# A mixture of experts: most experts' rows fetched by indirect DMA, the adds of gathered rows placed later, and the overflow loop moved between two experts

## The chip, the cores and the metric

One core of one Trainium2 chip runs the whole program. Time is device microseconds of one execution, median of three: 3032.44 us for the kernel before. The kernel computes two blocks of two layers each; the change lies in the second block's mixture of experts (MoE), which runs twice, once a layer.

## The reference

What matters is `grouped_moe`. Each of 512 tokens picks a group of 4 experts and in it the top 2 of 16; each expert is a gated feed-forward net on its own tokens, and each token gets the weighted sum of its two results.

```python
g_idx = jnp.argmax(jnp.max(grouped, axis=-1), axis=-1)
top_vals, top_idx = lax.top_k(in_group, TOP_K)
experts = g_idx[:, None] * EXPERTS_PER_GROUP + top_idx
weights = top_vals / jnp.sum(top_vals, axis=-1, keepdims=True)
...
xb = x_pad[buf_tok].reshape(n_blocks, EXPERT_BLOCK, D)      # blocks of 128 rows, one expert each
h = jax.nn.silu(xblk @ w_gate[e]) * (xblk @ w_up[e])        # 1024 -> 512
y = h @ w_down[e]                                           # 512 -> 1024
...
x = layer_norm(DEEPNORM_ALPHA * x + f, ln2_g[l], ln2_b[l])
```

All is f32. An expert's three weight matrices are 2 MB each.

## The kernel before

Every f32 operand of a matmul is split in two parts of a narrower format (a high part and the rest), and each product is three matmuls (`mm3`, L184 to L186): high times high, high times rest, rest times high. ACT makes the high part by a copy (L108 to L112, for weights L1616), DVE the rest by a subtraction (L123 to L128, for weights L1617). The tiles are named wh, wl, mh, ml for weights, xgh, xgl for tokens, hh, hl for the hidden layer.

`moe` (L1677) works through one layer. `route` has given each token's rank in each expert's list (`rank`), its two slots (`slotf`), and the list of overflow blocks (`ovi`): an expert holds 128 tokens; what doesn't fit goes into further blocks. First `moe` issues the loads of expert 0's and a part of expert 1's weights. Then a loop over the overflow blocks (`tc.For_i`, L1688) runs a whole expert per block, its weights chosen by a register; in the shown runs it runs zero times in layer 0 and once in layer 1. All engines branch there together. Then come the 16 experts:

- `expert_slots` makes one-hot matrices (tokens by slots) for two experts at a time, on DVE for the first pair and on POOL for the others (L1650).
- `expert_in` (L1629) multiplies the split tokens by the one-hots: 64 matmuls of 128x256 (L1639) give the transposed tokens of two experts, which are split into xgh and xgl.
- `expert_up` (L1653): 24 matmuls for gate, silu on ACT (L1659), 24 for up, the product hs on DVE (L1661), four transposes (L1664) and a split into hh, hl.
- `expert_down` (L1668), one expert behind: 24 matmuls, two output copies yo on ACT, and two stores of 256 KB into `yd` in DRAM, on ACT's queue.

Expert 15's down isn't stored; its result is added straight from the chip through the matrix `ct` (L1770). For the others, eight indirect DMAs on POOL (L1751) gather each token's two rows from `yd` into yg tiles, and DVE adds them with their weights (`add`, L1760) into f, which is x at first; some are done on PE through diagonals (L1768). `combine` (L1771) finishes a row, and the norm follows.

Weights come in tiles of 512 KB (`wload`, L1602, names mr and wr, nine buffers in all) on SP's queue, issued as buffers come free. `wsplit` (L1606) splits each. Pools of buffers: `t2` (26 tiles in the MoE, the fourth number of T2) for hidden tiles, outputs and splits; `f4` for one-hots, the loop's weights and gathered rows. The order of instructions on each engine is set by a scheduler, which reads dependences, buffers and the marks of `issue_after`.

## Time and profile before

| | us |
|---|---|
| median of three runs (3029.88 to 3035.55) | 3032.44 |
| the profiled execution, its own time | 3038.98 |
| its span in the profile | 3037.2 |
| expert stage of layer 0, from expert 0's first gate matmul to the last products | 329.24 |
| expert stage of layer 1, likewise | 332.57 |

The mean granted clock of TensorE was 0.981 of full speed. The page's second part cuts the span into 40 slices of 76 us; layer 0's experts are slices 22 to 26, layer 1's slices 36 to 40. PE is TensorE's matmuls, PEld its weight loads, which run beside them.

### The profile page before, as it was taken

What the parts mean: (1) busy time and instruction counts of PE and PEld (TensorE: products, weight loads), DVE (VectorE), ACT (ScalarE), POOL (GpSimd) and SP (SyncE); (2) the same over time, 40 slices, a digit from 0 to 9 for tenths busy, and PEclk for the clock granted to TensorE, in tenths of its full rate; (3) what the DMA queues carried; (4) which work ended last, traced back from release to release, by engine and by line L of the source; (5) the groups of instructions that cost most, each with busy time, mean ns of one, the idle gap of its engine ahead of it and who ended that gap; (6) DMA issues with size and microseconds to landing.
All of it is one profiled execution on the core that took longest, in us unless ns stands there. A gap on an engine that the chain in (4) does not pass through costs nothing. (4 is left out here: it accounts for less than half of the span.)

```text
span 3037.2 us, 44080 instructions
## 1 busy us (share of the span) xinstructions
PE 2896.9 (95%) x16635; PEld 2454.0 (81%) x16635; DVE 1951.3 (64%) x3817; ACT 1557.7 (51%) x2717; POOL 271.0 (9%) x282
## 2 busy tenths in 40 slices
PE   8999999999999999999989999879999999699996
PEld 6888878876669998878888888669987878588874
DVE  4454467576656776444477878978744345777788
ACT  4343377466655455223345777535542244476774
POOL 0000000000000000000027000440000000260023
PEclk9999999999999999999999999989999999899998
DMA  4242325431026222322365988931223335378996
GB/s 133 85 148 81 105 84 160 141 91 36 25 84 205 70 60 66 97 88 80 103 201 196 330 320 322 320 98 59 64 78 96 90 111 167 112 277 302 326 324 239
DMA packets 335599, 453.48 MB, mean 149 GB/s; under 512 B 24374, under 2 KB 208408, under 8 KB 335384
## 3 DMA queue, kind: packets, MB, share of 16 engines
q1 hardware_dynamic: 320856, 421.78, 42.1%
q10 hardware_dynamic: 12224, 20.46, 1.8%
q0 software_dynamic: 2304, 8.39, 0.8%
q8 instruction: 132, 2.16, 0.3%
q14 instruction: 83, 0.68, 0.1%
HBM read 421.69 MB, written 28.88 MB: 148 GB/s over the span
## 5 line engine op out<-in xcount | busy, mean ns | idle before, releaser
L164 DVE TENSOR_TENSOR wl<-wr,wh 128x1024 fp32r<-128x1024 f32 x348 | 422.9, 1217 | 441.1 <-ACT wh L163 436.9
L163 ACT CAST wh<-wr 128x1024 fp32r<-128x1024 f32 x352 | 363.1, 1033 | 579.9 <-PE pj L185 336.6
L184 PE MATMUL pj<-x,wh 128*128 128x512 f32 x1288 | 508.2, 395 | 0.6 <-ACT x L110 0.6
L185 PE MATMUL pj<-x,wh 128*128 128x512 f32 x1288 | 507.6, 394 | 0.0
L186 PE MATMUL pj<-x,wl 128*128 128x512 f32 x1288 | 506.3, 393 | 1.1 <-DVE wl L164 1.0
L186 PEld LDWEIGHTS pj<-x,wl 128*128 128x128 f32 x1288 | 241.9, 188 | 54.9 <-issue 4.7
L184 PEld LDWEIGHTS pj<-x,wh 128*128 128x128 f32 x1288 | 242.0, 188 | 52.6 <-issue 4.6
L185 PEld LDWEIGHTS pj<-x,wh 128*128 128x128 f32 x1288 | 242.0, 188 | 52.3 <-issue 5.6
L211 PE MATMUL pj<-wh,x 128*128 128x256 f32 x864 | 249.1, 288 | 3.8 <-DVE xb L277 3.1
L212 PE MATMUL pj<-wl,x 128*128 128x256 f32 x864 | 247.2, 286 | 0.0
L213 PE MATMUL pj<-wh,x 128*128 128x256 f32 x864 | 245.3, 284 | 0.0
L211 PE MATMUL pj<-wh,yh 128*128 128x256 f32 x640 | 181.6, 284 | 0.5 <-ACT wh L163 0.3
L212 PE MATMUL pj<-wl,yh 128*128 128x256 f32 x640 | 179.6, 281 | 1.5 <-DVE wl L164 1.5
L213 PE MATMUL pj<-wh,yl 128*128 128x256 f32 x640 | 179.1, 281 | 0.4 <-DVE yl L127 0.3
L211 PEld LDWEIGHTS pj<-wh,x 128*128 128x128 f32 x864 | 166.3, 193 | 5.2 <-DVE xb L277 3.5
L212 PEld LDWEIGHTS pj<-wl,x 128*128 128x128 f32 x864 | 166.6, 193 | 0.4
L213 PEld LDWEIGHTS pj<-wh,x 128*128 128x128 f32 x864 | 166.3, 193 | 0.3
L1639 PE MATMUL pt<-oh,x 128*128 128x256 f32 x1088 | 136.2, 287 | 18.4 <-DVE oh L1695 8.6
L1617 DVE TENSOR_TENSOR wl<-mr,wh 128x1024 fp32r<-128x1024 f32 x106 | 139.1, 1312 | 22.3 <-ACT wh L1616 22.2
L1639 PEld LDWEIGHTS pt<-oh,x 128*128 128x128 f32 x1088 | 135.3, 195 | 20.2 <-DVE oh L1695 8.7
L1617 DVE TENSOR_TENSOR ml<-mr,mh 128x1024 fp32r<-128x1024 f32 x108 | 135.9, 1258 | 21.5 <-ACT mh L1616 19.4
L1419 POOL TENSOR_TENSOR x<-x,bc 128x512 f32<-128x512 f32 x14 | 18.2, 1321 | 1255.7 <-ACT x L1328 1255.7
(503 smaller groups left out, 6607.0 us busy)
## 6 DMA issues: line engine op xcount, KB each, us to landing
wr<-in_w_in SPq DMA_DIRECT2D x124, 512.0 KB, 3.7
mr<-in_w_exp_gate SPq DMA_DIRECT2D x76, 512.0 KB, 6.6
mr<-in_w_exp_up SPq DMA_DIRECT2D x72, 512.0 KB, 5.5
mr<-in_w_exp_down SPq DMA_DIRECT2D x66, 512.0 KB, 5.9
wr<-in_w_exp_down SPq DMA_DIRECT2D x62, 512.0 KB, 6.3
wr<-in_hawk_w_in SPq DMA_DIRECT2D x60, 512.0 KB, 3.6
wr<-in_w_exp_up SPq DMA_DIRECT2D x56, 512.0 KB, 4.4
wr<-in_w_exp_gate SPq DMA_DIRECT2D x52, 512.0 KB, 6.9
```

The lines of the kernel that those rows point to most:

```text
L163: self.nc.scalar.copy(wh[:, :kt, :c], raw[:, :kt, :c])
L164: eng.tensor_tensor(wl[:, :kt, :c], raw[:, :kt, :c], wh[:, :kt, :c].bitcast(F32), op=OP.subtract)
L184: mm(ps, a[0], b[0], start=first, stop=False)
L185: mm(ps, a[0], b[1], start=False, stop=False)
L186: mm(ps, a[1], b[0], start=False, stop=last)
L211: mm(d, tok(x[k][0]), w[k][0][:, :n], start=k == 0 and a == 0, stop=False, skip_group_check=True)
L212: mm(d, tok(x[k][0]), w[k][1][:, :n], start=False, stop=False, skip_group_check=True)
L213: mm(d, tok(x[k][1]), w[k][0][:, :n], start=False, stop=end, skip_group_check=True)
L1419: getattr(nc, eng[0]).tensor_tensor(t[v], x[v], gb[0][v], op=OP.mult)
L1617: self.nc.vector.tensor_tensor(wl, raw, wh.bitcast(F32), op=OP.subtract)
L1639: nc.tensor.matmul(pt[:, u * n:(u + 1) * n], xs[i][part][:, f], oh[:, i], start=i == 0 and part == 0, stop=i == 3 and part == 1)
```

## The change

Only experts 0 and 1 still get their tokens by one-hot matmuls. For the others:

- `after_mix` also stores each finished row tile of x into DRAM (`x1d`, eight stores of 256 KB a layer, by `put`, L541, on SP's queue).
- `slot_tokens` turns the ranks into a list idx: for each slot and expert, the token's number. It takes small DVE operations, two iotas on POOL and eight small bf16 matmuls.
- `expert_fetch` gathers an expert's 128 rows from `x1d` by one indirect DMA on POOL (512 KB, two buffers xg), issued two experts ahead.
- `expert_turn` transposes them, eight f32 transposes of 128x128, and splits them.

Expert 15's one-hot, which `ct` needs, is still made, for that one expert, on POOL. The loop over overflow blocks stands between experts 1 and 2. The adds of gathered rows for the first two row tiles are held behind `mark`, the last split before them (expert 15's hl). `t2` in the MoE has 22 buffers instead of 26.

```diff
--- before.py
+++ after.py
@@ -39,7 +39,7 @@
 
 G, V = ("gpsimd", "gpsimd"), ("vector", "vector")
 AFFINE = ((G, G), (G, G)), ((G, G), (G, V))
-T2 = (26, 29, 45, 26)
+T2 = (26, 29, 45, 22)
 
 
 def slopes(n):
@@ -1418,6 +1418,7 @@
                 with self.tc.issue_after(self.ranked.ins) if late else nullcontext():
                     getattr(nc, eng[0]).tensor_tensor(t[v], x[v], gb[0][v], op=OP.mult)
                     getattr(nc, eng[1]).tensor_tensor(t[v], t[v], gb[1][v], op=OP.add)
+            self.put(self.x1d[l], i0 + a, t)
             h, lo = [self.wp.tile([P, D], F32R, name="x1", tag="xt", bufs=8) for _ in range(2)]
             x1[i0 + a] = h, lo
             for v in range(2):
@@ -1465,6 +1466,7 @@
                 if j:
                     nc.vector.tensor_tensor(s, s, rb, op=OP.add)
         self.yd = self.dp.tile([SLOTS, D], F32, name="yd")
+        self.x1d = [self.dp.tile([T, D], F32, name=f"x1d{l}") for l in range(2)]
 
     def clear_slots(self):
 
@@ -1642,13 +1644,64 @@
             xT += [(h[:, u * n:(u + 1) * n], lo[:, u * n:(u + 1) * n]) for u in range(2)]
         return xT
 
-    def expert_slots(self, rank, e, eng):
-
-        oh = self.f4(F32R, "oh").rearrange("p (i a s) -> p i a s", i=4, a=2)
-        for a in range(2):
+    def expert_slots(self, rank, e, n, eng):
+
+        oh = self.f4(F32R, "oh")[:, :4 * n * P].rearrange("p (i a s) -> p i a s", i=4, a=n)
+        for a in range(n):
             for i in range(4):
                 eng.tensor_scalar(oh[:, i, a], self.iota, rank[:, i, e + a:e + a + 1], None, op0=OP.is_equal)
         return oh.rearrange("p i a s -> p i (a s)")
+
+    def slot_tokens(self, ohs, rank):
+
+
+        nc = self.nc
+        tt = nc.vector.tensor_tensor
+
+        tok = self.small([2, 4, 16], name="tok", bufs=1)
+        for u in range(2):
+            nc.gpsimd.iota(tok[:, u], pattern=[[u * P, 4], [0, 16]], base=0, channel_multiplier=1 - u,
+                           allow_small_or_imprecise_dtypes=True)
+        ps = self.pt()
+        a = self.small([4, 16], name="sta", bufs=1)
+        r = self.small([2, 4], name="str", bufs=1)
+        tk = self.small([2, 4, 2, 16], BF16, name="stk", bufs=1)
+        at = self.ph.tile([P, 2, 4, P], BF16, name="at", tag="t2", bufs=self.bufs["t2"])
+        for j, oh in enumerate(ohs):
+            tt(a, oh, rank, op=OP.mult)
+            nc.vector.tensor_reduce(r[:, j], a, axis=AX.X, op=OP.add)
+            for u in range(2):
+                tt(tk[:, j, :, u], oh, tok[:, u], op=OP.mult)
+            for i in range(4):
+                nc.vector.tensor_scalar(at[:, j, i], self.iota, r[:, j, i:i + 1], None, op0=OP.is_equal)
+        for j in range(2):
+            for i in range(4):
+                nc.tensor.matmul(ps[:, :32], at[:, j, i], tk[:, j, i].rearrange("p u e -> p (u e)"),
+                                 start=j == 0 and i == 0, stop=j == 1 and i == 3)
+        idx = self.small([16], I32, name="idx", bufs=1)
+        hi = self.small([16], name="idh", bufs=1)
+        nc.vector.tensor_copy(hi, ps[:, 16:32])
+        tt(idx, ps[:, :16], hi, op=OP.add)
+        return idx
+
+    def expert_fetch(self, l, idx, e):
+
+        xg = self.ph.tile([P, D], F32, name="xg", tag="xg", bufs=2)
+        self.nc.gpsimd.indirect_dma_start(out=xg, out_offset=None, in_=self.x1d[l],
+                                          in_offset=bass.IndirectOffsetOnAxis(ap=idx[:, e:e + 1], axis=0))
+        return xg
+
+    def expert_turn(self, xg):
+
+        xT = []
+        for h4 in range(2):
+            pt = self.pt()
+            for k in range(4):
+                f = (4 * h4 + k) * P
+                self.nc.tensor.transpose(pt[:, k * P:(k + 1) * P], xg[:, f:f + P], self.ident)
+            h, lo = self.split(pt, 1.0, "xg")
+            xT += [(h[:, k * P:(k + 1) * P], lo[:, k * P:(k + 1) * P]) for k in range(4)]
+        return xT
 
     def expert_up(self, xT, wg, wu):
 
@@ -1684,33 +1737,41 @@
 
         cur = self.small([P], name="cur", bufs=1)
         nc.vector.tensor_scalar(cur, self.iota, 16.0 * P - 1.0, None, op0=OP.add)
-        nov = nc.values_load(ovi[0:1, 7:8], min_val=0, max_val=N_OV)
-        with tc.For_i(0, nov, 1) as b:
-            ev = nc.values_load(ovi[0:1, bass.ds(b, 1)], engines=[mybir.EngineType.SP], min_val=0, max_val=15)
-            row = b * P + 16 * P
-            we = [w[bass.ds(ev, 1)].rearrange("o k c -> (o k) c") for w in W]
-            oh = self.f4(F32R, "oh").rearrange("p (i a s) -> p i a s", i=4, a=2)
-            for i in range(4):
-                nc.vector.tensor_scalar(oh[:, i, 1], cur, slotf[:, 0, i:i + 1], None, op0=OP.is_equal)
-                nc.vector.scalar_tensor_tensor(oh[:, i, 0], cur, slotf[:, 1, i:i + 1], oh[:, i, 1].bitcast(F32),
-                                               op0=OP.is_equal, op1=OP.add)
-            nc.vector.tensor_scalar(cur, cur, float(P), None, op0=OP.add)
-            xT = self.expert_in(xs, oh.rearrange("p i a s -> p i (a s)"), 256)
-            hT = self.expert_up([[v[:, :P] for v in t] for t in xT], self.wrows(we[0], 8, True), self.wrows(we[1], 8, True))
-            self.expert_down(hT, we[2], self.yd[bass.ds(row, P)], True)
-        oh = self.expert_slots(rank, 0, nc.vector)
-        xT = self.expert_in(xs, oh, 256)
+
+        def overflow():
+            nov = nc.values_load(ovi[0:1, 7:8], min_val=0, max_val=N_OV)
+            with tc.For_i(0, nov, 1) as b:
+                ev = nc.values_load(ovi[0:1, bass.ds(b, 1)], engines=[mybir.EngineType.SP], min_val=0, max_val=15)
+                row = b * P + 16 * P
+                we = [w[bass.ds(ev, 1)].rearrange("o k c -> (o k) c") for w in W]
+                oh = self.f4(F32R, "oh").rearrange("p (i a s) -> p i a s", i=4, a=2)
+                for i in range(4):
+                    nc.vector.tensor_scalar(oh[:, i, 1], cur, slotf[:, 0, i:i + 1], None, op0=OP.is_equal)
+                    nc.vector.scalar_tensor_tensor(oh[:, i, 0], cur, slotf[:, 1, i:i + 1], oh[:, i, 1].bitcast(F32),
+                                                   op0=OP.is_equal, op1=OP.add)
+                nc.vector.tensor_scalar(cur, cur, float(P), None, op0=OP.add)
+                xT = self.expert_in(xs, oh.rearrange("p i a s -> p i (a s)"), 256)
+                hT = self.expert_up([[v[:, :P] for v in t] for t in xT], self.wrows(we[0], 8, True), self.wrows(we[1], 8, True))
+                self.expert_down(hT, we[2], self.yd[bass.ds(row, P)], True)
+
+        oh = self.expert_slots(rank, 0, 2, nc.vector)
+        xT = [[[v[:, a * P:(a + 1) * P] for v in t] for t in xT] for xT in [self.expert_in(xs, oh, 256)] for a in range(2)]
+        idx = self.slot_tokens((oh1, oh2), rank)
+        fetched = {e: self.expert_fetch(l, idx, e) for e in (2, 3)}
         hT = None
         f = []
         for e in range(16):
-            if e % 2 == 0 and e < 14:
-                oh = self.expert_slots(rank, e + 2, nc.gpsimd)
-                nx = self.expert_in(xs, oh, 256)
+            if e == 2:
+                overflow()
+            if e == 12:
+                oh = self.expert_slots(rank, 15, 1, nc.gpsimd)
+            if 0 < e < 15:
+                xT.append(self.expert_turn(fetched.pop(e + 1)))
+                if e < 13:
+                    fetched[e + 3] = self.expert_fetch(l, idx, e + 3)
             if e == 15:
                 self.expert_down(hT, W[2][14], self.yd[14 * P:15 * P])
-            o = e % 2 * P
-            h2 = self.expert_up([[v[:, o:o + P] for v in t] for t in xT],
-                                *[self.wrows(W[j][e], 8, first=first.pop(0) if first else None) for j in range(2)])
+            h2 = self.expert_up(xT[e], *[self.wrows(W[j][e], 8, first=first.pop(0) if first else None) for j in range(2)])
             if e == 2:
                 slot, wv, wl = self.weigh(oh1, oh2, sc, slotf)
             if e == 13:
@@ -1725,17 +1786,15 @@
             if 0 < e < 15:
                 self.expert_down(hT, W[2][e - 1], self.yd[(e - 1) * P:e * P])
             hT = h2
-            if e % 2:
-                xT = nx
 
         pt = self.pt()
         for i in range(4):
-            nc.tensor.transpose(pt[:, i * P:(i + 1) * P], oh[:, i, P:].bitcast(F32), self.ident)
+            nc.tensor.transpose(pt[:, i * P:(i + 1) * P], oh[:, i].bitcast(F32), self.ident)
         ct = self.t2(F32R, "ct")
         nc.scalar.copy(ct, pt)
         pw = self.pt()
         for i in range(4):
-            nc.tensor.matmul(pw[:, :1], oh[:, i, P:].bitcast(F32), wl[:, i:i + 1], start=i == 0, stop=i == 3)
+            nc.tensor.matmul(pw[:, :1], oh[:, i].bitcast(F32), wl[:, i:i + 1], start=i == 0, stop=i == 3)
         dg = self.t2(F32, "dg")
         for i in range(2):
             for j in range(2):
@@ -1771,13 +1830,15 @@
                 nc.vector.tensor_tensor(f[i][h], f[i][h], ps, op=OP.add)
 
         y = []
+        mark = self.split_end[0]
         for c in range(2):
             py = self.pj()
             ws2 = list(self.wsplit(raws[c]))
             if c:
-                for i in range(2):
-                    for j in range(2):
-                        add(i, j)
+                with tc.issue_after(mark.ins):
+                    for i in range(2):
+                        for j in range(2):
+                            add(i, j)
             for k, wk in enumerate(ws2):
                 self.mm3(py, hT[k], wk, k == 0, k == 3)
                 if c == 1 and k == 1:
```

SP's queue around the loop, layer 0, before (mr, wr: weight tiles; rovi: the register that holds the loop's count):

```order
L1602 DMA mr<-in_w_exp_up 128x2x512
L160 DMA wr<-in_w_mem_kv 128x4x256 x7
L1602 DMA wr<-in_w_exp_up 128x2x512 x3
L1687 TENSOR_LOAD rovi
L1687 ISA x2
L1602 DMA wr<-in_w_exp_gate 128x2x512
L1688 COMPARE_AND_BRANCH
L1688 UNCONDITIONAL_BRANCH x2
```

and now:

```order
L1604 DMA wr<-in_w_exp_down 128x2x512
L1604 DMA mr<-in_w_exp_down 128x2x512
L1604 DMA wr<-in_w_exp_down 128x2x512
L1604 DMA mr<-in_w_exp_gate 128x2x512
L1604 DMA wr<-in_w_exp_gate 128x2x512 x2
L1604 DMA mr<-in_w_exp_gate 128x2x512
L1604 DMA wr<-in_w_exp_up 128x2x512
L1604 DMA mr<-in_w_exp_up 128x2x512 x3
L1604 DMA wr<-in_w_exp_down 128x2x512
L1743 COMPARE_AND_BRANCH
L1743 UNCONDITIONAL_BRANCH x2
```

Before, the branch stands behind the first tiles of experts 0 and 1. Now it stands behind all loads of experts 0 and 1 that have a place and nine tiles more, which belong to expert 2 and to the down of expert 1.

PE where the loop's body ends (the first rows are the body's last), layer 1, before (x with a number: the parts of the tokens):

```order
L186 MATMUL pj<-mh,hl 128x512
L1688 REGISTER_ALU
L1688 COMPARE_AND_BRANCH
L1688 UNCONDITIONAL_BRANCH
L1639 MATMUL pt<-oh,x_24627 128x256
L1639 MATMUL pt<-oh,x_24628 128x256
L1639 MATMUL pt<-oh,x_24641 128x256
```

and now:

```order
L186 MATMUL pj<-mh,hl 128x512
L1743 REGISTER_ALU
L1743 COMPARE_AND_BRANCH
L1743 UNCONDITIONAL_BRANCH
L1701 MATMUL pt<-ident,xg 128x128 x8
L184 MATMUL pj<-wh,xgh 128x512
L185 MATMUL pj<-wl,xgh 128x512
L186 MATMUL pj<-wh,xgl 128x512
```

Before, the one-hot matmuls of experts 0 and 1 follow the loop; now the transposes of expert 3's fetched rows and the gate of expert 2 do.

DVE at the end of layer 1's experts (hs and hl: expert 15; yg: gathered rows; rw: weights of tokens), before:

```order
L1617 TENSOR_TENSOR wl<-mr,wh 128x1024
L1617 TENSOR_TENSOR ml<-mr,mh 128x1024
L1661 TENSOR_TENSOR hs<-hs,pj 128x512
L1617 TENSOR_TENSOR wl<-wr,wh 128x1024
L1617 TENSOR_TENSOR ml<-mr,mh 128x1024
L125 TENSOR_TENSOR hl<-pt,hh 128x512
L1745 COPY ws<-pt 128x1
L1760 SCALAR_TENSOR_TENSOR x<-yg,rw,x 128x512 x5
```

and now:

```order
L1619 TENSOR_TENSOR ml<-wr,mh 128x1024
L1619 TENSOR_TENSOR wl<-mr,wh 128x1024
L1819 SCALAR_TENSOR_TENSOR x<-yg,rw,x 128x512
L1714 TENSOR_TENSOR hs<-hs,pj 128x512
L1619 TENSOR_TENSOR ml<-mr,mh 128x1024
L1619 TENSOR_TENSOR wl<-wr,wh 128x1024
L125 TENSOR_TENSOR hl<-pt,hh 128x512
L1804 COPY ws<-pt 128x1
L1619 TENSOR_TENSOR ml<-mr,mh 128x1024
L1819 SCALAR_TENSOR_TENSOR x<-yg,rw,x 128x512 x3
```

Before, all adds stand behind hs, hl and ws. Now one add of gathered rows stands ahead of hs, and the others as before behind it; the same holds in layer 0. This one belongs to the third row tile, which the mark doesn't hold.

## Rows read from the trace of the kernel before

**Rows 1.** The page: busy time by engine, and slices of PE and DMA.

```profile
PE 2896.9 (95%) x16635; PEld 2454.0 (81%) x16635; DVE 1951.3 (64%) x3817; ACT 1557.7 (51%) x2717; POOL 271.0 (9%) x282
...
PE   8999999999999999999989999879999999699996
...
DMA  4242325431026222322365988931223335378996
```

**Rows 2.** Windows of both expert stages: us, busy by engine, clock, DMA share, GB/s.

```profile
core 0: us, PE busy (x) PEld busy (x) DVE busy (x) ACT busy (x) POOL busy (x), PEclk, DMA share, GB/s
1634.18:1963.42 329.24, 324.11 (x1618) 268.88 (x1616) 270.36 (x254) 239.89 (x278) 63.10 (x47) 0.99 0.90 319
2671.06:3003.63 332.57, 325.94 (x1618) 270.51 (x1616) 270.39 (x254) 239.73 (x278) 65.96 (x52) 0.99 0.89 316
```

**Rows 3.** Timeline of ACT, silus of four experts: start, us, operation.

```profile
1676.18 0.60 ACT L1659 ACTIVATE hs<-pj 128x512 f32<-128x512 f32 x1 [0.33 <-PE pj L186]
1693.29 0.60 ACT L1659 ACTIVATE hs<-pj 128x512 f32<-128x512 f32 x1 [0.33 <-PE pj L186]
1717.94 0.60 ACT L1659 ACTIVATE hs<-pj 128x512 f32<-128x512 f32 x1 [0.33 <-PE pj L186]
1735.06 0.60 ACT L1659 ACTIVATE hs<-pj 128x512 f32<-128x512 f32 x1 [0.32 <-PE pj L186]
```

**Rows 4.** The page's group of L1639, and PE's timeline: eight transposes in layer 1.

```profile
L1639 PE MATMUL pt<-oh,x 128*128 128x256 f32 x1088 | 136.2, 287 | 18.4 <-DVE oh L1695 8.6
...
2595.78 1.07 PE L1497 MATMUL pt<-ident,x 128*128 128x128 f32 x8
```

**Rows 5.** Layer 0 at the loop: timelines of PE and DVE, and the loop's branches.

```profile
1612.06 0.28 PE L213 MATMUL pj<-wh,mx 128*128 128x256 f32 x1
1617.62 0.80 PE L1639 MATMUL pt<-oh,x 128*128 128x256 f32 x2 [5.28 <-ACT mh L1616]
...
1613.44 1.72 DVE L1650 TENSOR_SCALAR oh<-iota,rank 128x128 fp32r<-128x128 f32 x8 [4.08 <-ACTq L1688]
...
L1688 PEldq COMPARE_BRANCH  x6: 86/192/3861, 1610.8 to 2652.5; - x6
```

**Rows 6.** Timeline of PE in layer 1: the body's start and what follows it.

```profile
2619.09 8.28 PE L1639 MATMUL pt<-oh,x 128*128 128x256 f32 x48 [8.59 <-DVE oh L1695]
...
2653.89 6.38 PE L1639 MATMUL pt<-oh,x 128*128 128x256 f32 x35 [4.50 <-DVE oh L1650]
```

**Rows 7.** Timeline of ACT and DVE in layer 0: one weight tile's split.

```profile
1637.16 1.05 ACT L1616 CAST mh<-wr 128x1024 fp32r<-128x1024 f32 x1 [0.33 <-PE pj L186]
...
1638.24 1.23 DVE L1617 TENSOR_TENSOR ml<-wr,mh 128x1024 fp32r<-128x1024 f32 x1
```

**Rows 8.** DMA issues: count, KB each, median us to landing.

```profile
mr<-in_w_exp_gate SPq DMA_DIRECT2D x76, 512.0 KB, 6.6
...
yd<-yo ACTq DMA_DIRECT2D x62, 256.0 KB
```

**Rows 9.** Windows inside the expert stages, columns as in rows 2.

```profile
1676.18:1717.94 41.76, 41.76 (x217) 35.21 (x216) 33.49 (x33) 30.98 (x36) 0.00 (x0) 1.00 0.91 326
1720.00:1755.00 35.00, 35.00 (x188) 29.72 (x188) 28.86 (x29) 25.72 (x31) 0.00 (x0) 1.00 1.01 367
1815.00:1840.00 25.00, 25.00 (x143) 21.67 (x142) 19.23 (x19) 17.11 (x21) 0.00 (x0) 1.00 1.01 366
1925.00:1945.00 20.00, 20.00 (x90) 16.13 (x90) 15.61 (x15) 15.37 (x20) 0.00 (x0) 1.00 1.05 385
2860.00:2880.00 20.00, 20.00 (x121) 17.62 (x120) 15.13 (x16) 13.37 (x17) 0.00 (x0) 1.00 1.03 386
```

**Rows 10.** The indirect DMAs of L1751: ns on POOL (min/median/max), and landing.

```profile
L1751 POOL DMA_INDIRECT yg<-yd,rslot x16: 933/1014/2107, 1949.2 to 3004.4; - x16
...
DMA to landing us min/median/max: 5.2/5.8/8.3
```

**Rows 11.** Timelines of POOL and DVE: third gather and expert 15's hs, both layers.

```profile
2992.66 1.97 POOL L1751 DMA_INDIRECT yg<-yd,rslot  x1 [0.30 <-issue]
...
2994.06 0.69 DVE L1661 TENSOR_TENSOR hs<-hs,pj 128x512 f32<-128x512 f32 x1 [0.25 <-PE pj L186]
...
1953.58 0.94 POOL L1751 DMA_INDIRECT yg<-yd,rslot  x1 [0.30 <-issue]
...
1953.85 0.69 DVE L1661 TENSOR_TENSOR hs<-hs,pj 128x512 f32<-128x512 f32 x1 [0.25 <-PE pj L186]
```

## The prediction

> **What bounds the kernel now.** I read the page first: TensorE is busy for 95% of the span [rows 1]. The two expert stages are the two stretches in which DMA is busy too, digits 8 and 9 of slices 23 to 26 and 37 to 39. Next the windows by stage: each expert stage lasts about 330 us, PE works in all but 5 to 7 us of it, and the 16 DMA engines are busy 0.90 and 0.89 of it at 319 and 316 GB/s [rows 2]. So PE sets the end there, with the weight stream close behind. The starts of the silu of four experts in a row give the price of a step: 17.11 us when no one-hot group lies between two of them, 24.65 when one does [rows 3]. The 64 matmuls of expert_in for two experts thus cost 24.65 − 17.11 = 7.54 us of PE, all on the path.
>
> **What goes and what comes on PE.** Of 8 groups a layer the first (experts 0 and 1) stays and 7 go: 7 × 7.54 = 52.8 us. In their place come 14 expert_turn of 8 transposes of 128x128. The same shape took 1.07 us for 8 in layer 1 [rows 4], so 14 × 1.07 = 15.0. Net −37.8 a layer, **−75.6** in all. The transposes' weight loads lie beside them (PEld is busy less than PE, [rows 1]). The splits of xg need 2 ops of 512 columns per expert instead of 4 per pair: no change on DVE or ACT. POOL's one-hots go but for 4 ops a layer; nobody waited for them between the experts (PE stands 5 to 7 us in a whole stage, [rows 2]).
>
> **The loop, moved.** It now stands where a stream runs. Layer 0 skips it. Today the skip costs 5.28 us of idle PE between the last mem_kv matmul and the first L1639, 3.86 of which is PE's own branch [rows 5]; the one-hots of 1.72 us start in it. After, PE runs from mem_kv into expert_in but still waits some 1.5 us for one-hots: −3.8. At the new place PE drains (about 1.6: a copy of 0.6, as a silu of [rows 3], and 1 for the meeting at the branch, an estimate: the first matmul behind the body waited 4.50 in layer 1 for that meeting and its one-hots together, [rows 6]), branches (3.9), turns expert 3, and waits for the first split of weights, which ACT and DVE can't do ahead of their own branches: an ACT copy of 1.05 and a DVE op of 1.23, about 2.3 [rows 7]. Then it runs at the lower clock: after its gap the first 48 matmuls of L1639 in layer 1 took 8.28 us, 172 ns each against 7.54 / 64 = 118 between the experts [rows 6], for which I add 1. That is +8.8 − 3.8 = **+5** (bounds +1, branch and refill hidden, to +9, nothing saved at the top). In layer 1 the body runs once. It takes 34.8 us from 2619.09 to 2653.89 [rows 6] wherever it stands; the 4.50 us behind it, a wait for one-hots, turns into the refill; the drain and the entry come new: **+4** (+1 to +8). SP's nine prefetches (eight tiles of expert 2's gate and up and one of down 1) stand ahead of its branch, so the prefetch survives the loop.
>
> **The weight stream.** Behind the loop PE has 332.6 (layer 1's window, [rows 2]) − 52.8 − 28.5 (two ups and one down are 5/3 of 17.11, done before) + 13.9 (13 turns) = 265 us to do. The last tile may land some 8 us before its end (a split and one down), so it has 257, with the refill about 259. In that time go 163 tiles of 512 KB, 29 stores of 256 KB and 11 fetches of 512 KB: 163 × 0.524 + 29 × 0.262 + 11 × 0.524 = 98.8 MB [rows 8]. That is 381 GB/s, where today's mean is 319. Can DMA do it? In stretches where its share reaches 1 it moved 366 and 367, and 385 and 386 in the best 20 us [rows 9]. I take 372, nearer the longer stretches: 98.8 / 0.372 = 265.6, **+6** a layer, +12 in all (0 at 386; +19 a layer at 355, below). So the forecast is that DMA becomes the bound behind the loop, at 7.34 MB a step (12 tiles, 2 stores, a fetch) / 0.372 = 19.7 us, where PE alone would need 17.11 + 1.07 = 18.2.
>
> The Trainium skill ("DMA: Bandwidth & Descriptors", section "Where 436 GB/s comes from") says that for transfers between HBM and SBUF a limit of about 358 GB/s binds. At 358 the term above would be 98.8 / 0.358 = 276, +17 instead of +6 a layer. The trace shows 385 and 386 over 20 us [rows 9], which is more than that limit, so I don't use it. Another page of the Trainium skill ("HBM Reference", its first section) has a core that streams alone well above its share, at about 425; at that rate the term would be nothing, and no stretch of this trace shows it.
>
> **The fetches.** Two buffers and an issue two experts ahead give each fetch some 36 us; an indirect DMA of today is at most 2.1 on POOL and 8.3 to landing [rows 10]. Only the first is tight: its index needs slot_tokens (some 22 small DVE ops between splits, 8 small matmuls), and turn 2 stands right behind expert 0's hidden transposes, some 11 us into expert 0. I take +1.5 a layer (0 to +4), **+3**. The small ops themselves and the 8 stores of x1d on SP: +0.5 a layer, **+1** (0 to 4); SP's queue has nothing urgent behind those stores.
>
> **The tail.** Before, every add of gathered rows stood behind expert 15's hl split. After, the hoisted adds of tokens 0 and 1 are held behind it, but one of the others, the first gather of token block 2, now stands on DVE ahead of expert 15's hs multiply, in both layers. That gather is the third on POOL: issued at 2992.66, and 5.2 us or more to land [rows 10, 11], so 2997.9 at the earliest, while hs started at 2994.06. Behind the waiting add on DVE stand hs and its splits; PE waits for hs with its transposes and the last down. In layer 0 the third issue is at 1953.58 and hs at 1953.85 [rows 11]. The wait costs about 4.5 to 5.5, of which one add of 0.7 comes back and some is covered by PE's backlog: **+4** a layer (0 to +7), +8.
>
> **Sum.** −75.6 + 9 + 12 + 3 + 1 + 8 = −42.6. Against the profiled execution's own 3038.98 that is 2996.4; that execution stood 6.5 above the median, and on the median's scale 3032.44 − 42.6 = **2990**.
>
> **Rivals.** (A) DMA keeps up and PE stays the bound. For it: 385 and 386 have been reached, and nine tiles lie ahead. Without the 12 and with half of tail and fetch: −75.6 + 9 + 1 + 5.5 = −60, so 2972. (B) DMA settles lower: the whole stages moved 319 at a share of 0.90, and 319 / 0.90 = 354, 326 / 0.91 = 358 [rows 2, 9]. At 355: 98.8 / 0.355 = 278, +19 instead of +6 a layer, so 3016. The limit of about 358 that the Trainium skill states ("DMA: Bandwidth & Descriptors", "Where 436 GB/s comes from") would give 3012. (C) Slower: the stream behind the loop gets no more than today's mean, since stores, fetches and loads then share queues and the buffers come free in bursts. The place is experts 2 to 15, the price 98.8 / 0.326 − 259 = 44 a layer, so 3032.4 − 42.6 − 12 + 88 = 3066. It decides below the rate at which the gain is gone: 27.3 a layer to lose, 98.8 / (259 + 27.3) = 345 GB/s. Against it: every stretch with share 1 was above 360. (D) The change doesn't do what it says: the prefetch behind the loop or the fetches come late at every turn. 28 waits of 1.5 us would eat the 42, near 3030. The lead of 36 us speaks against it.
>
> **How the numbers follow.** Main case 0.57 (2975 to 3005), A 0.13, B 0.15, C 0.09, D 0.06. The range runs from 2964, A with nothing lost in the tail, to 3018, just above B; C, D and a little of the rest are outside. About 0.2%, 6 us, is what a measurement can tell from no change: faster by more 0.86 (main, A, B and a little of D), within it 0.05, slower 0.09.
>
> **What would show it.** L1639's successor should have 192 matmuls (two groups and the body's) instead of 1088 [rows 4], and L1701 224 transposes near 0.13 us each. The silu starts behind the loop tell the bound: 18.2 us a step is A, 19.7 is the forecast, 20.9 (today's pair divided by two, 41.76 / 2, [rows 9]) is no gain. In the window from the loop to the end, DMA's share should be near 1 at 370 GB/s and PE should wait for splits whose raw tile has just landed; if the share stays at 0.9 and PE still idles, another engine is the bound and the DMA term is wrong. PE should idle about 8 us at the loop in layer 0. In the tail the add ahead of hs should wait for a gather, 4 to 5 us; if hs isn't late, that term goes. PE waiting at many turns for xg would make the prediction wrong, as would a rate below 345 GB/s.

## The result

The changed kernel takes 2988.01 us, median of four runs (2980.78 to 2988.76), beside 3031.85 of the kernel before: a ratio of 0.9849 (0.9831 to 0.9867), 44 us less. In a second set of runs it had 0.9846 (0.9830 to 0.9862). The forecast was 2990. That it came so near is partly luck: three costs of its sum (the loop, the stream, the fetches) were too large and two (the transposes, the tail) too small, and the step that was to take 19.7 us takes 18.4 to 18.7.

The page of the changed kernel, to be read beside [rows 1], and windows inside layer 0's experts, beside [rows 9]:

```profile
span 2978.8 us, 42692 instructions
PE 2830.5 (95%) x15979; PEld 2369.2 (80%) x15979; DVE 1947.0 (65%) x3853; ACT 1543.0 (52%) x2713; POOL 199.0 (7%) x210
...
DMA  4242324431016312323266999832122334479995
```

```profile
core 0: us, PE busy (x) PEld busy (x) DVE busy (x) ACT busy (x) POOL busy (x), PEclk, DMA share, GB/s
...
1695.00:1760.00 65.00, 64.91 (x300) 52.24 (x299) 56.98 (x57) 51.99 (x63) 3.27 (x3) 1.00 1.05 393
1760.00:1855.00 95.00, 94.87 (x435) 74.92 (x434) 84.51 (x82) 77.80 (x93) 4.68 (x5) 1.00 1.05 393
1855.00:1900.00 45.00, 41.91 (x184) 31.90 (x182) 40.88 (x35) 33.21 (x41) 16.81 (x8) 1.00 0.99 362
```

PE lost 66 us of work. Where 326 GB/s went before, 393 go now for 160 us on end, at a share of 1.05, and PE still has no idle time there. The kernel before reached such a rate too, but only briefly. The 385 and 386 of [rows 9] are not its best 20 us; a window that begins a little before the last row there has more (columns as above):

```profile
2857.50:2877.50 20.00, 20.00 (x117) 17.39 (x116) 16.20 (x16) 14.58 (x18) 0.00 (x0) 1.00 1.04 394
```

In the last of the changed kernel's three windows PE stops for 3 us and the rate falls: that is the stretch in which POOL adds the two parts of x.

A table of the same stretches in three executions, from the starts of silus, of the routing's first small matmul, and the end of the last product of `ct`:

| us | before | changed | changed, second profile |
|---|---|---|---|
| layer 0: routing to expert 2's silu | 81.4 | 68.5 | 71.4 |
| expert 2's silu to expert 15's | 272.4 | 249.6 | 249.1 |
| expert 15's silu to the last product | 29.5 | 32.6 | 34.3 |
| layer 0's last product to layer 1's routing (the handover) | 632.0 | 631.7 | 632.4 |
| layer 1: routing to expert 2's silu | 103.0 | 94.7 | 94.4 |
| expert 2's silu to expert 15's | 275.7 | 251.4 | 253.0 |
| expert 15's silu to the end of the span | 48.5 | 60.1 | 59.0 |

The profiled execution of before stood 7.1 us above the median of 3031.85, the changed kernel's first 7.2 below its own, so their spans differ by 58.4 us, 14 more than the medians. The second profile (span 2984.7) stands nearer its own median of 2988.80. Differences of 2 or 3 us in one row are within what one build shows of itself.

Steps in the middle, to be read beside [rows 3] (timeline of ACT, experts 11 to 13 of layer 0):

```profile
1824.11 0.60 ACT L1712 ACTIVATE hs<-pj 128x512 f32<-128x512 f32 x1 [0.29 <-PE pj L186]
1842.73 0.60 ACT L1712 ACTIVATE hs<-pj 128x512 f32<-128x512 f32 x1 [0.27 <-PE pj L186]
1861.35 0.60 ACT L1712 ACTIVATE hs<-pj 128x512 f32<-128x512 f32 x1 [0.38 <-PE pj L186]
```

18.62 us each, where a pair took 41.77 before, 20.9 each. The three steps from expert 7 to 10 took 18.36 to 18.40.

The turn itself, where PE goes from an expert's down to the next gate (timeline of PE):

```profile
1798.31 0.39 PE L186 MATMUL pj<-mh,hl 128*128 128x512 f32 x1
1798.54 1.04 PE L1701 MATMUL pt<-ident,xg 128*128 128x128 f32 x8
1799.33 0.48 PE L184 MATMUL pj<-wh,xgh 128*128 128x512 f32 x1
1799.65 0.39 PE L185 MATMUL pj<-wl,xgh 128*128 128x512 f32 x1
```

The tail, beside [rows 11] (timeline of DVE, layer 0 and layer 1):

```profile
1917.52 1.00 DVE L1819 SCALAR_TENSOR_TENSOR x<-yg,rw,x 128x512 f32<-128x512 f32 x1 [5.24 <-DMA yg<-yd,rslot]
1918.44 0.68 DVE L1714 TENSOR_TENSOR hs<-hs,pj 128x512 f32<-128x512 f32 x1
...
2930.50 0.75 DVE L1819 SCALAR_TENSOR_TENSOR x<-yg,rw,x 128x512 f32<-128x512 f32 x1 [7.46 <-DMA yg<-yd,rslot]
2931.17 0.68 DVE L1714 TENSOR_TENSOR hs<-hs,pj 128x512 f32<-128x512 f32 x1
```

The add ahead of hs does wait for its gather, 5.24 and 7.46 us, and hs stands right behind it.

### The profile page after: what moved, and what is told of

Same layout as the page of the kernel before. It is cut to its first block, busy times and chain, and to the rows that moved or that the text cites. A ratio compares the mean times of both kernels' runs of the same rounds, so it can differ in the third digit from the quotient of the medians.

```text
span 2978.8 us, 42692 instructions
## 1 busy us (share of the span) xinstructions
PE 2830.5 (95%) x15979; PEld 2369.2 (80%) x15979; DVE 1947.0 (65%) x3853; ACT 1543.0 (52%) x2713; POOL 199.0 (7%) x210
## 3 DMA queue, kind: packets, MB, share of 16 engines
q1 hardware_dynamic: 323160, 425.98, 42.6%
## 5 line engine op out<-in xcount | busy, mean ns | idle before, releaser
L211 PE MATMUL pj<-wh,x 128*128 128x256 f32 x864 | 248.0, 287 | 1.5 <-DVE xb L277 0.7
L1619 DVE TENSOR_TENSOR ml<-mr,mh 128x1024 fp32r<-128x1024 f32 x108 | 134.0, 1242 | 26.3 <-ACT mh L1618 25.6
L1619 DVE TENSOR_TENSOR wl<-mr,wh 128x1024 fp32r<-128x1024 f32 x106 | 131.6, 1242 | 27.4 <-ACT wh L1618 27.2
L1618 ACT CAST mh<-mr 128x1024 fp32r<-128x1024 f32 x108 | 113.0, 1048 | 26.2 <-PE pj L186 9.8
L1618 ACT CAST wh<-mr 128x1024 fp32r<-128x1024 f32 x106 | 111.4, 1051 | 23.9 <-DMA mr<-in_w_exp_down 8.6
L212 PEld LDWEIGHTS pj<-wl,yh 128*128 128x128 f32 x640 | 121.2, 189 | 2.4 <-DVE wl L164 1.9
```

What stands on the lines that cost most here:

```text
L211: mm(d, tok(x[k][0]), w[k][0][:, :n], start=k == 0 and a == 0, stop=False, skip_group_check=True)
L212: mm(d, tok(x[k][0]), w[k][1][:, :n], start=False, stop=False, skip_group_check=True)
L1618: self.nc.scalar.copy(wh, raw)
L1619: self.nc.vector.tensor_tensor(wl, raw, wh.bitcast(F32), op=OP.subtract)
```

## Experiments

### Is the weight stream the bound? Twice the fetches, and almost none

The edit of double_fetch, in `expert_fetch`:

```diff
         self.nc.gpsimd.indirect_dma_start(out=xg, ..., in_offset=...(ap=idx[:, e:e + 1], axis=0))
+        self.nc.gpsimd.indirect_dma_start(out=xg, ..., in_offset=...(ap=idx[:, e:e + 1], axis=0))
```

> The changed kernel with every fetch of an expert's rows issued twice into the same buffer: 0.52 MB more per expert, nothing more for PE, DVE or ACT. Theory A, the weight stream is the bound in the steady experts, at 394 GB/s: a step goes from 7.34 MB / 394 = 18.6 us to 7.86 / 394 = 20.0, and the 10 or so steps of each layer that the tiles ahead don't cover give 10 to 14 us a layer, 20 to 30 in all, near 3013. At the rate that the prediction took, 372, a step would be 21.1. Theory B, PE is the bound and the step is 18.4 to 18.6 because the transposes cost more there than in layer 1's router: steps stay at 18.6 and the time within 4 us of 2988.

It took 3030.79 us, 0.9988 of before (0.9979 to 0.9997): nearly all of the gain is gone. A window in the middle of layer 0 (columns as above), and PE's timeline at its first turn:

```profile
1790.00:1860.00 70.00, 66.54 (x301) 50.86 (x300) 58.76 (x57) 53.40 (x64) 9.75 (x7) 1.00 1.05 395
```

```profile
1639.65 1.94 PE L1703 MATMUL pt<-ident,xg 128*128 128x128 f32 x8 [7.37 <-DMA xg<-x1d,idx]
```

The seven steps from expert 6 to 13 take 19.2 to 20.7 us, 19.9 on the mean, and the rate is 395 GB/s. So the stream runs at its own limit, and a step that moves 7.86 MB is as long as that takes. Theory A holds for the steps, in mechanism and number: from expert 2's silu to 15's a layer takes 12 us more. Its total, near 3013, is missed by 18 us, because it left out the start. The second row shows that: the first turn (the eight transposes of `expert_turn`) waits 7.37 us for its doubled fetch, and the start grows by 8 to 12 us a layer. In the changed kernel this first fetch just comes in time: the step from expert 0 to 1 is 11.57, that is 10.60 of before and a turn, and in its second profile the first turn of layer 0 waits 0.33.

reuse_rows leaves out the rows of experts 4 to 15:

```diff
-                xT.append(self.expert_turn(fetched.pop(e + 1)))
-                if e < 13:
-                    fetched[e + 3] = self.expert_fetch(l, idx, e + 3)
+                xT.append(self.expert_turn(fetched[2 + (e + 1) % 2]))
```

> The changed kernel without the fetches of experts 4 to 15: their transposes read the rows of experts 2 and 3 again, so the rows of 12 experts are left out and their results are those of other tokens. PE, DVE and ACT do the same work; 0.52 MB less moves per expert. Theory A, the stream at 394 GB/s binds: 6.82 / 394 = 17.3 us a step is less than PE's own, so steps fall from 18.6 to 18.2, by 3 to 5 us a layer, 6 to 10 in all, near 2980. Theory B, PE binds: steps stay at 18.4 to 18.6 and the time within 3 us.

It took 2977.93 us, 0.9819 (0.9801 to 0.9837), some 9 us less than the changed kernel, with intervals that overlap by a little. The profile is clearer (timeline of ACT, layer 0):

```profile
1806.08 0.60 ACT L1712 ACTIVATE hs<-pj 128x512 f32<-128x512 f32 x1 [0.40 <-PE pj L186]
1824.45 0.60 ACT L1712 ACTIVATE hs<-pj 128x512 f32<-128x512 f32 x1 [0.39 <-PE pj L186]
1842.82 0.60 ACT L1712 ACTIVATE hs<-pj 128x512 f32<-128x512 f32 x1 [0.39 <-PE pj L186]
1861.18 0.60 ACT L1712 ACTIVATE hs<-pj 128x512 f32<-128x512 f32 x1 [0.40 <-PE pj L186]
```

18.37, 18.37, 18.36: the step with no transfer in its way. Against 18.62, which is 7.34 MB / 394 GB/s, the two limits lie 0.25 us apart, and the changed kernel stands on both: its steps of 18.36 to 18.40 in layer 0 are those of reuse_rows, its steps of 18.62 those of the stream.

And a turn costs PE 18.37 − 17.11 = 1.26 us, not 1.07. In the rows of the turn above, the eight transposes take 0.79 us until the next matmul, and the one behind that comes 0.09 late. A further 0.23 is a wait three microseconds into the gate behind it (changed kernel, timelines of DVE and PEld):

```profile
1799.85 1.29 DVE L125 TENSOR_TENSOR xgl<-pt,xgh 128x512 fp32r<-128x512 f32 x2 [0.26 <-ACT xgh L112]
1801.31 1.23 DVE L1619 TENSOR_TENSOR wl<-wr,wh 128x1024 fp32r<-128x1024 f32 x1 [0.17 <-ACT wh L1618]
...
1802.59 0.19 PEld L185 LDWEIGHTS pj<-wl,xgh 128*128 128x128 f32 x1 [0.41 <-DVE wl L1619]
```

The splits of the turned rows (xgh on ACT, xgl on DVE) stand ahead of a weight tile's, and PE's weight load waits for that tile; the matmuls there follow each other at 0.37 and 0.34 us instead of 0.23. The same wait stands in the steps of reuse_rows. The remaining 0.15 is that the 72 matmuls of a step follow each other at 0.234 us on the mean, in the kernel before at 0.232; why is not shown.

### The loop: back on top, and moved alone

loop_top calls `overflow()` ahead of experts 0 and 1 in the changed kernel:

```diff
+        overflow()
         oh = self.expert_slots(rank, 0, 2, nc.vector)
...
-            if e == 2:
-                overflow()
```

> The changed kernel with the loop over overflow blocks back ahead of experts 0 and 1; everything else as changed. The prediction's term: the move costs 9 us (5 in layer 0, 4 in layer 1), so this should be 9 faster, near 2979. Reading the two traces from the routing matmul to expert 2's silu gives another figure: 0.2 us of cost in layer 0 and 4.7 in layer 1, so about 5 faster. Rival: at the top, the loop keeps the weight stream waiting at its branch with ten tiles in place, where the moved loop lets it run on for nine more tiles; then experts 2 to 15 meet a later stream and this is 5 to 15 us slower than the changed kernel.

2988.35 us, 0.9855 (0.9840 to 0.9871): no difference, so neither the 5 to 9 us less nor the 5 to 15 us more that were expected. The profile shows both halves: from the routing to expert 2's silu it is 2.3 and 1.2 us shorter, from there to expert 15's 1.5 and 2.7 longer. The handover, which the edit doesn't touch, is 5.4 us longer (637.1); under adds_held below is where that lies. So the total hides some 5 us, and the run doesn't weigh the move to the last us.

loop_only makes the same move in the kernel before:

```diff
-        nov = nc.values_load(...)
-        with tc.For_i(0, nov, 1) as b: ...
...
         for e in range(16):
+            if e == 2:
+                overflow()
```

> The kernel before with one edit: the loop over overflow blocks between experts 1 and 2. Nothing is fetched; one-hot matmuls and adds are those of before. Theory A, the prediction's term: the move costs 9 us by itself (drain, branch, refill and the lower clock in layer 0, drain and entry in layer 1), so about 3043 against 3034 of before. Theory B, from the kernel with the loop back on top, where the start until expert 2's silu got 2.3 and 1.2 us shorter and experts 2 to 15 got 1.5 and 2.7 longer: the move costs 3 to 4 us at the start and gives them back only where the weight stream binds; here PE binds, so 3 to 5 us slower, about 3038.

3048.41 us, 1.0044 (1.0032 to 1.0056): 13 us slower than before, more than either theory gave. Layer 0 behind the loop (timelines of PE and POOL):

```profile
1663.21 10.48 PE L1639 MATMUL pt<-oh,x 128*128 128x256 f32 x64 [9.62 <-POOL oh L1650]
...
1658.34 12.48 POOL L1650 TENSOR_SCALAR oh<-iota,rank 128x128 fp32r<-128x128 f32 x17 [43.95 <-SPq L1690]
```

PE waits 9.62 us for POOL, whose one-hots can't run ahead of POOL's branch. The starts grow by 7.1 and 8.7 us. In the changed kernel no one-hot stands there. What PE does first behind the loop is already on the chip (timeline of PE, layer 0):

```profile
1646.29 0.39 PE L186 MATMUL pj<-mh,hl 128*128 128x512 f32 x1
1650.00 1.33 PE L1701 MATMUL pt<-ident,xg 128*128 128x128 f32 x5 [3.33 <-SPq L1743]
```

So the move is dear by itself and cheap with the fetch: 3.33 us of idle PE, and 0.75 left at the top, in place of the 5.28 of [rows 5].

fetch_only takes both moves back: the loop on top as above, and the adds without the mark.

```diff
-                with tc.issue_after(mark.ins):
-                    for i in range(2):
-                        for j in range(2):
-                            add(i, j)
+                for i in range(2):
+                    for j in range(2):
+                        add(i, j)
```

> The changed kernel with the loop back on top and without the mark on the adds: only the fetch of rows and what serves it is left of the change. Theory A, the fetch carries the whole gain and the two moves together weigh nothing, as each taken back alone showed (0.9855 and 0.9833 of before, against 0.9849): 0.983 to 0.986 of before, 2985 to 2993. Theory B, the moves help each other: then this is off by more than 6 us to one side.

2983.17 us, 0.9822 (0.9808 to 0.9836). Theory A's range was 0.983 to 0.986, so it is just outside, on the fast side, and its interval touches that of the changed kernel beside it (0.9830 to 0.9862). The fetch carries the whole gain. Whether the two moves cost 5 us or nothing these runs don't settle, the less so as the handover took 636.5 us here.

### The adds

no_mark takes only the mark away (the diff above without the loop).

> The changed kernel without the mark that holds the adds of row tiles 0 and 1. In its order two adds then stand ahead of expert 15's hs on DVE instead of one, and they wait for other gathers than the third alone. Theory A, what counts is the wait of the last gather ahead of hs: if it is the third again, hs stays 10 to 12.5 us behind its silu and the time is 2988 within 3; if it is a later one, each further place on POOL is 1.25 us later. Theory B, the number of adds ahead counts: one more add of 0.7 us and one more wait, 2 to 6 us slower.

2984.99 us, 0.9833 (0.9820 to 0.9846): no difference that can be told. hs starts 9.7 and 9.6 us after its silu, against 10.1 and 12.5, though two adds stand ahead of it. Only the first of them waits, 4.28 and 4.18 us, and for the first gather, not for the third; the second finds its rows there. So what counts is the gather that is waited for, as theory A said, and not the number of adds.

adds_held puts the other two adds behind the mark:

```diff
-        for i in range(2, 4):
-            add(i, 0)
+        with tc.issue_after(mark.ins):
+            for i in range(2, 4):
+                add(i, 0)
```

> The changed kernel with one edit: the two adds of row tiles 2 and 3 that don't go through PE are held behind the same mark as the others, expert 15's hl split. In the changed kernel's trace, hs of expert 15 starts 10.1 us after its silu in layer 0 and 12.5 in layer 1, where the kernel before needs 5.3 in both; the difference is DVE waiting 5.24 and 7.46 for a gather in front of that add. Theory A, the wait is lost time: hs comes 5.3 us after the silu again and the kernel gets 5 to 12 us faster, near 2980 against 2988. Theory B, the gathers decide the end anyway, so the wait only moves to the adds behind hl or to the products of the diagonals: hs comes early, but silu to last product stays at 32.2 and 35.0 us, and the time moves by less than 3 us.

2990.24 us, 0.9859 (0.9844 to 0.9874): no gain. Yet hs comes 5.6 and 5.4 us after its silu again, and silu to last product falls from 32.6 and 35.4 to 27.8 and 28.4. A part of the gain is given back outside: the handover took 638.8 us instead of 631.7. Some six of these seven us arise in its first 40, where PE waits for xb, the input of the next layer's first products (timelines of PE in the changed kernel, adds_held and loop_top; the rows start 27.6, 32.1 and 32.7 us behind the last product):

```profile
1968.52 0.39 PE L211 MATMUL pj<-wh,x 128*128 128x256 f32 x1 [0.75 <-DVE xb L277]
...
1972.39 0.58 PE L211 MATMUL pj<-wh,x 128*128 128x256 f32 x1 [3.10 <-DVE xb L277]
...
1972.19 0.58 PE L211 MATMUL pj<-wh,x 128*128 128x256 f32 x1 [6.32 <-DVE xb L277]
```

Behind these rows the granted clock of the next 10 us is 1.00, 0.78 and 0.83. The order of SP's weight loads, which the edit also changed there, is not the cause: loop_top has the changed kernel's order and the long handover, no_mark the order of adds_held and 633.2 us. Which change of order makes PE wait is not shown; the long handover comes with some builds, whatever their edit is about.

held_l1 holds them in layer 1 only (`if l else nullcontext()`), so that the handover keeps its order.

> The changed kernel with the two adds of row tiles 2 and 3 held behind the mark in layer 1 only; layer 0 and the start of the stages behind it keep the changed kernel's order. With both layers held, silu to last product fell by 4.7 and 7.0 us, but the weight loads and splits at the handover from layer 0 stood in another order and the stretch from layer 0's last product to layer 1's routing grew by 7.1. Theory A, that order ate the gain: here the handover is the changed kernel's (631.7 us), the tail of layer 1 is 7 us shorter, and the time 5 to 8 us less, near 2981. Theory B, the handover differs from run to run whatever the order: then it is 632 or 638 here by chance and the median stays near 2988.

2987.66 us, 0.9846 (0.9834 to 0.9859): no gain either, and theory A falls. The handover took 634.4 us here, between the two. hs is early, 5.36 us after its silu, but from silu to last product it is 33.0, not 28.4. Timelines of DVE and PE, layer 1:

```profile
2928.69 0.69 DVE L1714 TENSOR_TENSOR hs<-hs,pj 128x512 f32<-128x512 f32 x1
...
2938.99 2.58 DVE L1819 SCALAR_TENSOR_TENSOR x<-yg,rw,x 128x512 f32<-128x512 f32 x3 [4.40 <-DMA yg<-yd,rslot]
...
2942.28 1.22 PE L1829 MATMUL pj<-yll,ct 128*128 128x512 f32 x2 [4.38 <-DVE yll L127]
```

The wait has moved behind hl, to the next add whose gather isn't there, and yll, a part of expert 15's result that PE needs, stands behind that add on DVE. The gathers themselves are late: in the changed kernel's layer 1 the first one starts 3.1 us after expert 15's silu, before 0.2 (in layer 0 0.6 in both, in the second profile 2.4 and 2.6). The last store into `yd` is issued 5.3 us ahead of that silu in both kernels, so 8.4 us pass from it to the first gather here, and 5.5 before. That the full DMA queues delay this store is an inference from these times; no run took it apart.

### Two ways to start the sums without POOL

load_x_held, on top of held_l1:

```diff
-                            nc.gpsimd.tensor_tensor(f[i][h], xs[i][0][:, o].bitcast(F32), xs[i][1][:, o].bitcast(F32), op=OP.add)
+                            nc.sync.dma_start(f[i][h], self.x1d[l][i * P:(i + 1) * P, o])
```

> As the kernel before it in this list, and x as the start of the sums is loaded back from its copy in DRAM (8 loads of 256 KB a layer on SP) instead of being summed from its two parts on POOL. In the changed kernel the last two steps take 22.3 and 24.7 us; a step has 18.4 us of PE work, and the last holds the down of expert 14 too, 5.6 more, 24.0. DVE's splits are the slow ones there while POOL sums. Theory A, POOL's sums slow DVE: the step of expert 14 falls from 22.3 to about 19 and that of 15 to 24, 3 to 4 us a layer, 7 in all, near 2974. Theory B, the stream is the bound: 2.1 MB more at 394 GB/s cost 5.3 us a layer, so nothing is gained or 4 us lost.

2979.36 us, 0.9818 (0.9805 to 0.9831), 8 us less than held_l1. Both theories are half right: expert 14's step falls from 22.3 to 18.4 and 17.9, and expert 15's rises from 24.7 to 26.7 and 29.3, behind 2.1 MB more.

x_on_pe needs no load:

```diff
-                            nc.gpsimd.tensor_tensor(f[i][h], xs[i][0][:, o].bitcast(F32), xs[i][1][:, o].bitcast(F32), op=OP.add)
...
-                nc.vector.scalar_tensor_tensor(f[i][h], gs[2 * i + j][:, half[h]], wv[:, j, i:i + 1], f[i][h],
+                nc.vector.scalar_tensor_tensor(f[i][h], gs[2 * i + j][:, half[h]], wv[:, j, i:i + 1],
+                                               f[i][h] if j else xs[i][0][:, half[h]].bitcast(F32),
...
+                nc.tensor.matmul(ps, self.ident, xs[i][1][:, half[h]].bitcast(F32), start=True, stop=False)
```

> The changed kernel without POOL's sums of x's two parts: DVE's first add of gathered rows starts from the high part, and PE adds the low part in the products that finish a row tile, by 8 matmuls of 128x512 a layer against the identity, 0.47 us each. With x loaded back by DMA, the step of expert 14 fell from 22.3 to 18.4 and 17.9, but that of expert 15 rose from 24.7 to 26.7 and 29.3, since the loads stand in front of the last weights. Theory A, POOL's sums slow DVE's splits and are the only reason for the 22.3: here that step is 18.4 to 18.9 and the last 24 to 24.7, 4 us a layer, and since no add stands ahead of hs any more the tail loses 2 to 7 more, minus up to 2 for the matmuls: 2972 to 2982. Theory B, the stream or the gathers take up what the steps lose: the tail grows by as much, and the time is 2985 or more.

2973.40 us (2964.23 to 2974.86), 0.9786 of before (0.9768 to 0.9804): faster than both kernels, 15 us less than the changed kernel's 2988.80 in the same set, and inside theory A's range. (The other products of a row tile lose their start flag, and the two halves summed on PE alone take the high part in their last add.) Why is read from DVE's splits (groups of DVE by form: busy, mean ns, idle before), first the changed kernel from 1860 to 1900 us, then x_on_pe from 1865 to 1905:

```profile
L1619 DVE TENSOR_TENSOR ml<-wr,mh 128x1024 fp32r<-128x1024 f32 x4 | 8.2, 2040 | 0.0
L1619 DVE TENSOR_TENSOR wl<-mr,wh 128x1024 fp32r<-128x1024 f32 x5 | 7.0, 1408 | 0.0
```

```profile
L1619 DVE TENSOR_TENSOR ml<-wr,mh 128x1024 fp32r<-128x1024 f32 x4 | 4.9, 1219 | 0.8 <-ACT mh L1618 0.8
...
L1619 DVE TENSOR_TENSOR wl<-mr,wh 128x1024 fp32r<-128x1024 f32 x6 | 7.3, 1222 | 0.7 <-ACT wh L1618 0.6
```

While POOL sums, from 1864 to 1881, the same split takes 1.4 to 2.0 us on the mean instead of 1.22, and DVE, which has no idle time in these 17 us, sets the step. Taken one by one, seven of the eight splits beside the sums take 1.70 to 2.32 us and one 1.21, and those before and behind 1.21 to 1.23. The kernel before has this too: there the splits take 1.69 to 2.32 us from 1904 to 1922, and expert 14's step 22.46. So this loss is older than the change, and a part of these 15 us may lie in the kernel before as well; no run took the sums out of it.

Without the sums the step of expert 14 is 18.4 in both layers and that of 15 23.3. No add stands ahead of hs either, and in layer 1 the span ends 53.6 us behind expert 15's silu, against 59.0 and 60.1. In the changed kernel's layer 1 PE stands idle for 7.85 us ahead of expert 15's hidden transposes, and from 10 to 35 us behind the silu its granted clock is 0.78 on the mean; here PE has no such wait, and the clock is 1.00. The handover was a long one again (636.7), so the 15 us are not a best case.

### The buffers, and the changed kernel again

t2_22 is the kernel before with `T2 = (26, 29, 45, 22)`.

> The kernel before with 22 buffers in t2 during the experts instead of 26, nothing else. The prediction left this edit at nothing: an expert takes 9 of them a step, and 22 are more than two steps' worth. Expected within 3 us of before. Rival: outputs and splits wait for buffers; the steps of 17.1 and 24.65 us grow and the time by 5 us or more.

3035.30 us, 0.9996 (0.9986 to 1.0007): the smaller pool costs nothing that can be told.

And the changed kernel once more, without an edit:

> The changed kernel once more, beside the others on one chip. Expected 0.983 to 0.987 of before. In the profile: the stretch from silu 2 to silu 15 at 249 to 252 us a layer, silu 15 to the last product at 32 to 36; the start and the handover between the layers vary by up to 7 us from one build's execution to another, and this tells how much of that one build shows by itself.

2988.80 us, 0.9846 (0.9830 to 0.9862). The table above has its stretches: 249.1 and 253.0 in the middle, the second 1 us above what was expected, and 34.3 at the end of layer 0 as expected. Its handover took 632.4 us, near the first profile's 631.7, so the 636.5 to 638.8 of four other builds are not what one build shows of itself.

## Why the prediction was right

**Work taken from PE.** Right in kind, a little too good: the counts are the 192 one-hot matmuls and 224 transposes that were named, 52.8 us a layer go, and the turns cost 14 × 1.26 = 17.6 instead of 15.0. Net −70.4 in all, not −75.6. The row of 8 transposes was read by its busy time; what a turn costs is the step with it less the step without it. "No change on DVE or ACT" counted their work rightly and missed its place: the split of the turned rows now stands where PE waits 0.23 us behind it.

**The loop.** Predicted +9. From the routing to expert 2's silu, PE's own change is two groups out and two turns in, −12.6. Measured: −12.9 and −10.0 in layer 0's two profiles, −8.3 and −8.6 in layer 1's. So the move cost 0 to 3 and 4, some 4 to 7. Layer 0's 5 was the part mis-sized: its branch of 3.86 us, taken from [rows 5], was not met again in the changed kernel (its longest branch of PE took 0.33, though loop_only has one of 3.07), and PE idled 3.33 (4.51 in the second profile) where I had 8. The lower clock behind this gap is there: it was granted 0.61 on the mean from 1650 to 1654 us.

**The stream.** Predicted as the bound behind the loop at 372 GB/s, +12. It is a bound, but at 393 to 395, and it lies so close to PE's own step that it costs little. By the sign that the prediction itself named, 18.2 us a step for rival A and 19.7 for the forecast, the measured 18.4 to 18.7 speak for A. Against the 248.0 and 247.9 us of reuse_rows, which has no stream in the way, the middle stretch is 1.1 to 1.6 us longer in layer 0 and 3.5 to 5.2 in layer 1, so +5 to +7. The step that was off is "I take 372, nearer the longer stretches". In the 35 us of [rows 9] that gave 367 the loads waited for buffers, so their rate was no measure of what the queues can carry. SP's waits in the kernel before, 1720 to 1755 us, and in the changed kernel, 1760 to 1855 (total us, times, longest):

```profile
SPq L1602 <- DVE ml L1617: 16.4, 11, 2.8
SPq L1602 <- DVE wl L1617: 4.3, 6, 1.0
...
SPq L1604 <- DMA yd<-yo: 24.2, 10, 3.7
SPq L1604 <- DMA mr<-in_w_exp_gate: 11.1, 12, 1.0
```

Before, SP waited for DVE's splits, which free the buffers; now nearly all of its waits, 65 of 71 us, end with the landing of a transfer. The trace of before did show the higher rate, 394 for 20 us; the windows of [rows 9] were set beside it. Nor is a share of 1 the top: it goes to 1.05, and by that 319 GB/s at 0.90 would be 372, not the 354 of rival B (an estimate from these rows). By mechanism the truth lies between the forecast and its rival A, nearer to A. Rivals B and C needed rates of 355 and less than 345 in that stretch and fall. The Trainium skill ("DMA: Bandwidth & Descriptors", "Where 436 GB/s comes from") lets about 358 GB/s bind between HBM and SBUF; this case's trace disagrees, with 393 for 160 us on end. What another page of the Trainium skill ("HBM Reference", first section) states for a core that streams alone, about 425, isn't contradicted; no run here reached it.

**The fetches.** Right, and rival D with its late fetches falls: no turn waits in the changed kernel's steady steps, and the first comes just in time, as double_fetch shows by breaking it. The +3 for it was too much, by 2 or 3. The +1 for small operations and stores of x was measured by no run on its own.

**The tail.** Right in place and mechanism (the add ahead of hs waits for the third gather), too small in size: +3.0 and +4.8 in layer 0, and in layer 1 +11.6 and +10.5 to the end of the span, some 14 to 16 in all against +8. What I had not seen is that the gathers of layer 1 start later too, that the next add on DVE waits in turn, and that PE's granted clock falls behind such waits, so that taking the wait away in layer 1 alone gave nothing back that could be measured.

**The sum.** −70.4 + 5 + 6 + 15 = −44, and the measured difference of medians is 44; the prediction's −42.6 was made of other parts, and its errors, some +5 and +7 against −4, −6 and −2, cancelled by luck. This sum leaves out two longer steps of before that went with the one-hots (25.6 and 28.9 us instead of 24.65, 5 us together), and the executions differ by about as much, so it is not to be read to the last us.

## What to carry to other kernels

Replacing matmuls by a gather paid here because DMA had room (a share of 0.90, where 1.05 can be reached) and the fetch could be issued two steps ahead; compute both steps, PE's and the stream's, and take the rate from a run that is truly starved (here one with extra bytes), not from hand-set windows of a kernel that another engine bounds; where only such a kernel is at hand, move the window along and ask what SP waited for. A control-flow meeting in mid-stream costs what can't be prepared on its far side: check for each engine what it must make anew behind its branch. An elementwise job that is hidden on POOL may still slow the engine that is nearly the bound. And read a small difference by stretches before explaining it by the edit: a part of the kernel that the edit doesn't touch moved by 5 to 7 us here from build to build.

## What was not expected of the hardware

With extra bytes the 16 DMA engines held 395 GB/s over 70 us, where the kernel before moved 319 and 316 over a stage and 394 in its best 20 us. POOL's additions of 128x512 f32 stretched DVE's subtractions of 128x1024 from 1.22 to 2.04 us on the mean of four; they do not share data. DVE's operations that read a result of PE (`pt`, `pj`) were not stretched beside the same additions (hs and hl took 0.68 us). PE's branch at a loop that runs zero times took 3.86 us in the kernel before, 3.07 in loop_only, 1.28 in loop_top and no more than 0.33 in the changed kernel; what makes the difference is not shown.
